# A squared-ReLU MLP in eight steps, with its two projections interleaved on TensorE

## The chip, the cores and the metric

The kernel runs on one core of one Trainium2 chip. The metric is the device time of one execution in microseconds (us); less is better. Engines are named as in the profile: PE (TensorE, matrix products), PEld (its weight loads), DVE (VectorE), ACT (ScalarE), POOL (GpSimd) and SP (SyncE, which issues the weight loads from memory).

## What is computed

A decoder trunk of two layers on 256 rows of 2,048 values, in float32. The change concerns the MLP, which each layer has once:

```python
D_MODEL = 2048; SEQ = 256; D_FF = 4 * D_MODEL          # 8,192 hidden values

def sq_relu_mlp(u, w_up, w_down):
    return jnp.square(jax.nn.relu(u @ w_up)) @ w_down

# in each layer, after the convolution or attention sub-layer:
u = rmsnorm(h, mlp_pre_g[i])
h = h + rmsnorm(sq_relu_mlp(u, mlp_w_up[i], mlp_w_down[i]), mlp_post_g[i])
```

Layer 0 has a gated short convolution ahead of its MLP, layer 1 a stick-breaking attention. These parts are the same in both kernels.

## The kernel before

**Float32 by parts.** Each operand is split into a rounded high part and the rest, its low part. A product of two operands takes three TensorE products: high x high, high x low and low x high. Weights come from memory in chunks of 128 x 1,024 (`raw`, four buffers, loads issued by SP). ACT rounds a chunk to `whi` (L144) and DVE subtracts to get `wlo` (L155). High and low parts go round in a ring of seven buffers each (`RING`), so a chunk's parts can be made ahead of PE by as much as the ring holds: a new part waits until PE has done with the one seven places before.

**Who sets the order.** PE executes the products in the order in which the program writes them. For DVE and ACT a scheduler decides the order when the kernel is built, except around the norms between sub-layers, where it is written out. An engine executes its instructions strictly in that order. On-chip result memory has eight banks of 128 x 512 values, and the building layer keeps two engines from touching one bank at the same time by adding waits.

**Up projection, by tiles.** `up` makes hidden tiles of 128 hidden values x 256 rows. For each of 16 blocks of the inner dimension there is one high product (L927: weights' high part, against the high and low parts of the input side by side, 512 columns) and one low product (L940: weights' low part against the input's high part, 256 columns, added to the first half of the bank). When a tile's 32 products are done, `hidden` copies the second half of the bank with ACT (`half`, L873), adds it to the first half with DVE (`s`, L875), and applies ReLU and square on ACT (L876, L877). The result is split into `hid` parts (L228, L229). Even tiles run all high products and then all low ones, odd tiles the other way round; the banks rotate over all eight. The first six tiles of an MLP (`LEAD_UP`) advance together, block by block.

**Down projection, by units.** For each 128 hidden values, and each half of the output columns, there are two row blocks x two column blocks of 512, three TensorE products each (`Group.half`, L281 to L283). `Mixed` replaces some pairs of neighbouring blocks of hidden values by a scheme with seven instead of eight products of sub-blocks (each three TensorE products; L348 to L350). It needs differences of the weights (`split_seven`, four DVE subtractions, L181), so that three and a half chunks are split for such a pair in place of two, and sums of the hidden tiles (`sums_of`). Four extra banks (`more`) collect products that belong to several outputs. When a group ends, ACT copies them out (L997) and nine accumulating DMAs issued by GpSimd (L989) add them to the output sums `mg`; in the last quarter DVE adds them (`combined`).

**The staging.** An MLP goes in four quarters of 2,048 hidden values. A quarter first makes all its 16 hidden tiles, then runs the down projection for both column halves. `PAIRS` names the pairs that take seven products: four for each column half in three quarters, two in the last. At the end of each quarter the sums are added to `mg` in memory on chip (L982, L984).

Of the kernel before, what the change touches and what calls it, by code (L numbers as in the profile page):

```python
# [14 lines left out]
P = 128  # L15
D = 2048
T = 256
# [29 lines left out]
QUARTERS = FF // D  # L47
PAIRS = ([(2, 5, 8, 11)] * 2, [(2, 5, 8, 11)] * 2, [(2, 5, 8, 11)] * 2, [(2, 6)] * 2)
APART = 11
# [10 lines left out]
UP_FIRST = lead_then_rows(list(range(KD)), LEAD_UP)  # L60
UP_ORDER = lead_then_rows(list(range(KD)), 0)
# [6 lines left out]
def trunk(ctx, tc, x, xT, vecs, rows, ws, out):  # L68
# [237 lines left out]

    class Mixed(Group):

        def __init__(self, first, xs, banks, evict, sums, extra, combine, pool, pairs):
            super().__init__(first, KD, xs, banks, evict)
            self.sums, self.extra, self.combine, self.pairs = sums, extra, combine, pairs
            self.more = None  # L320
            for i in pairs:
                sevens[first + i] = pool

        def both(self, i):
            if i in self.pairs:
                self.seven(i)
            elif i - 1 not in self.pairs:
                super().both(i)

        def seven(self, i):  # L330
            b11, b21, b22, t1, t2, t3, t4 = chunk(self.first + i)
            if self.more is None:
                self.more = [bank(n, "more") for n in self.extra]
            s1, more = self.sums[i]

            def x(k, b):
                return [part_of(self.xs, i + k, b, j) for j in range(2)]

            def sums(j):
                return [t[:, (j - 1) * P : j * P] for t in more] if j else s1  # L340

            p1, p5, p6, p7 = self.more
            for ps, (xh, xl), (hi, lo), own in (
                (p1, x(0, 0), b11, True), (self.ps[0, 0], x(1, 0), b21, False), (self.ps[0, 1], sums(3), b22, False),
                (p5, sums(0), t1, True), (p6, sums(1), t2, True), (p7, sums(2), t3, True),
                (self.ps[1, 0], x(1, 1), t4, False),
            ):
                nc.tensor.matmul(ps[:], xh, hi, start=own and i == self.pairs[0], stop=False)  # L348
                nc.tensor.matmul(ps[:], xh, lo, start=False, stop=False)  # L349
                nc.tensor.matmul(ps[:], xl, hi, start=False, stop=own and i == self.pairs[-1])  # L350
            if i == self.pairs[-1]:
                self.combine(*self.more)
            spent(UNIT * 7 / 4)
            spent(UNIT * 7 / 4)
# [338 lines left out]
    def mlp_weights(i):  # L693
        for q in range(QUARTERS):
            W["up", i, q] = Weights(ws[f"up{i}{q}"])
            W["dn", i, q] = Weights(ws[f"dn{i}{q}"])
# [168 lines left out]
    def mlp(pool, i, before, after):  # L865
# [5 lines left out]
        def hidden(xs, n, ps, sums, pairs):  # L871
            half = pool.tile([P, T], F32, tag="half", name="half", bufs=2)
            nc.scalar.activation(half[:], ps[:, T:], AF.Copy)  # L873
            s = pool.tile([P, T], F32, tag="s", name="s", bufs=3)
            nc.vector.tensor_tensor(s[:], ps[:, :T], half[:], op=ALU.add)  # L875
            nc.scalar.activation(s[:], s[:], AF.Relu)  # L876
            nc.scalar.activation(s[:], s[:], AF.Square)  # L877
            if xs[n // 4] is None:
                xs[n // 4] = operand("hid4")
            if n in pairs and n != APART:  # L880
                two_parts([part_of(xs, n, 0, j) for j in range(2)], s[:, :P])
            else:
                split_tile(xs, n, s[:])
            if n in pairs:
                held[n] = s
            elif n - 1 in pairs:
                sums[n - 1] = sums_of(xs, n - 1, held.pop(n - 1), s)

# [5 lines left out]
        def sums_of(xs, n, x, y):  # L894

            t = after.dump()
            s1, s2, s3, s4 = (t[:, j * P : (j + 1) * P] for j in range(4))
            a11, a21, a12, a22 = x[:, :P], x[:, P:], y[:, :P], y[:, P:]
            for to, u, v, op in (
                (s1, a21, a22, ALU.add), (s2, s1, a11, ALU.subtract),  # L900
                (s3, a11, a21, ALU.subtract), (s4, a12, s2, ALU.subtract),
            ):
                nc.vector.tensor_tensor(to, u, v, op=op)
            if n == APART:
                one = pool.tile([P, 2 * P], F32R, tag="s1", name="sums", bufs=1)
                one = [one[:, j * P : (j + 1) * P] for j in range(2)]
            else:
                one = [part_of(xs, n, 1, j) for j in range(2)]
            more = pool.tile([P, 6 * P], F32R, tag="hg", name="sums", bufs=4)
            more = [more[:, j * 3 * P : (j + 1) * 3 * P] for j in range(2)]  # L910
            two_parts(one, s1)
            two_parts(more, t[:, P:])
            return one, more

        def up(q, xs, sums, pairs):
            w = W["up", i, q]
            order = UP_FIRST if q == 0 else UP_ORDER
            place = {kn: m for m, kn in enumerate(order)}
            pss = {}

            def high(k, n, b=None, begin=True, end=False):

                if n not in pss:
                    pss[n] = bank((n + 2) % 8, "up")
                ps, x = pss[n][:].rearrange("p (a b t) -> p a b t", a=2, b=NB), u[k // 4][:, k % 4]
                if b is None:
                    nc.tensor.matmul(  # L927
                        ps, weight(0, k, n), x, start=begin and k == 0, stop=end and k == KD - 1, skip_group_check=end
                    )
                else:  # L930
                    nc.tensor.matmul(ps[:, :, b, :], weight(0, k, n), x[:, :, b, :], start=k == 0 and b == 0, stop=False)  # L931
                if end and k == KD - 1:
                    hidden(xs, n, pss.pop(n), sums, pairs)
                spent(TILE_HIGH if b is None else TILE_LOW)

            def low(k, n, begin=False, end=True):
                if n not in pss:
                    pss[n] = bank((n + 2) % 8, "up")
                x = u[k // 4][:, k % 4, 0].rearrange("p b t -> p (b t)")
                nc.tensor.matmul(  # L940
                    pss[n][:, :T], weight(1, k, n), x, start=begin and k == 0, stop=end and k == KD - 1,
                    skip_group_check=begin,
                )
                if end and k == KD - 1:
                    hidden(xs, n, pss.pop(n), sums, pairs)
                spent(TILE_LOW)

            def weight(part, k, n):
                m = place[k, n]
                return chunk(w.base + m // CH, part == 1)[part][:, m % CH * P : (m % CH + 1) * P]  # L950

            def tiles_of(kns):
                for k, n in kns:
                    high(k, n)
                for k, n in kns:
                    low(k, n)

            lead = list(range(LEAD_UP if q == 0 else 0))
            if lead:
                first = [(k, n) for k in range(ALONE) for n in lead]  # L960
                for b in range(NB):
                    for k, n in sorted(first, key=lambda kn: (kn[0] // 4, kn[1] // 3 if kn[0] < 4 else 0)):
                        high(k, n, b)
                for k, n in first:
                    low(k, n)
                for k in range(ALONE, KD):
                    tiles_of([(k, n) for n in lead])
            for n in range(len(lead), KD):
                if n % 2 == 0:
                    tiles_of([(k, n) for k in range(KD)])  # L970
                else:
                    for k in range(KD):
                        low(k, n, True, False)
                    for k in range(KD):
                        high(k, n, None, False, True)

        def add(q, j, c, b, ps, adds):
            r = part[b][2 * j + c]
            with tc.high_priority():
                if r is None:  # L980
                    r = part[b][2 * j + c] = result()
                    nc.scalar.activation(r, ps[:], AF.Copy)  # L982
# [4 lines left out]
            elif b and c:  # L987
                for first, second in adds:
                    nc.gpsimd.dma_start(first(), second, accum_op=ALU.add)  # L989
# [323 lines left out]
```

## Time and profile before

| | |
|---|---|
| Time, median of three runs | 2140.67 us (2140.43 to 2142.43) |
| Profiled execution | 2141.22 us, span of its trace 2139.5 us |
| Granted TensorE clock | 0.999 |
| Busy: PE, DVE, ACT, POOL | 99%, 73%, 63%, 5% of the span |
| Memory traffic | 194 GB/s read over the span |

The profile is one execution taken by the hardware profiler. Its groups give a line of the kernel, an engine, an operation, its output and inputs, a count, then busy time and the mean duration in ns, then the idle time before it and what ended that. Products on PE overlap: a product of 512 columns is listed with some 390 ns although the next may start earlier, so slots are read from the distance of starts. A list of waits gives total time, times and longest.

### The profile page before, as it was taken

How to read it: one execution, taken by the hardware profiler on the slowest of the kernel's cores; microseconds unless marked ns; L12 is line 12 of the kernel's file. 1: busy time of each engine (PE TensorE's matmuls, PEld its weight loads, DVE VectorE, ACT ScalarE, POOL GpSimd, SP SyncE). 2: the span in 40 equal slices, each digit the busy share in tenths (PEclk: the TensorE clock that was granted, in tenths of full speed). 3: DMA queues.
4: the chain of work that ended last, by engine and by line, in shares of the span. 5: the costliest groups of instructions: out<-in, count | busy, mean ns of one | idle time of the engine just before them, and what ended most of it. 6: DMA issues, size and time to landing. Idle time of an engine off the chain costs nothing.

```text
span 2139.5 us, 29677 instructions
## 1 busy us (share of the span) xinstructions
PE 2128.4 (99%) x10906; PEld 1822.7 (85%) x10906; DVE 1572.3 (73%) x2243; ACT 1340.6 (63%) x2010; POOL 100.1 (5%) x121
## 2 busy tenths in 40 slices
PE   9999999999999999999999999999999999999998
PEld 8888888888888888888888888889888888888886
DVE  8766655888679679768866777558886797687677
ACT  7545444766666666665567888547666666666654
POOL 0000000001101101100000000000011011011000
PEclk9999999999999999999999999999999999999999
DMA  8655664659858858965575445655588589569663
GB/s 306 216 187 187 189 234 145 218 178 257 247 175 248 263 171 243 268 207 171 176 231 168 158 158 171 214 166 188 183 250 261 172 236 276 186 205 287 213 198 121
DMA packets 130321, 445.54 MB, mean 208 GB/s; under 512 B 14592, under 2 KB 14848, under 8 KB 129152
## 3 DMA queue, kind: packets, MB, share of 16 engines
q1 hardware_dynamic: 113472, 408.65, 58.7%
q0 software_dynamic: 16416, 34.61, 8.3%
q8 instruction: 85, 1.39, 0.3%
q14 instruction: 60, 0.49, 0.1%
q10 hardware_dynamic: 288, 0.39, 0.1%
HBM read 413.19 MB, written 2.10 MB: 194 GB/s over the span
## 4 chain that ended last, share of the span: by engine, by line
PE 97%; ACT 1%; DVE 1%; DMA 1%; issue 0%; SPq 0%; DVEq 0%; ACTq 0%
PE up L927 21%; PE acc L281 12%; PE acc L283 12%; PE acc L282 12%; PE up L940 11%; PE acc L750 11%; PE more L348 2%; PE more L349 2%; PE more L350 2%; PE acc L348 2%; PE acc L349 2%; PE acc L350 2%; PE lead L750 2%; PE up L931 1%; PE tr L234 1%
## 5 line engine op out<-in xcount | busy, mean ns | idle before, releaser
L155 DVE TENSOR_TENSOR wlo<-raw,whi 128x1024 fp32r<-128x1024 f32 (+1 forms) x566 | 676.5, 1210 | 294.1 <-ACT whi L144 248.1
L144 ACT ACTIVATE whi<-raw 128x1024 fp32r<-128x1024 f32 (+1 forms) x566 | 590.6, 1048 | 296.8 <-PE acc L283 123.6
L927 PE MATMUL up<-u,whi 128*128 128x512 f32 x1952 | 458.3, 390 | 0.0
L927 PEld LDWEIGHTS up<-u,whi 128*128 128x128 f32 x1952 | 361.6, 188 | 71.7
L940 PEld LDWEIGHTS up<-u,wlo 128*128 128x128 f32 x2048 | 255.9, 191 | 5.8
L940 PE MATMUL up<-u,wlo 128*128 128x256 f32 x2048 | 259.0, 283 | 0.0
L281 PE MATMUL acc<-whi,hid 128*128 128x512 f32 x576 | 224.2, 389 | 0.0
L283 PE MATMUL acc<-whi,hid 128*128 128x512 f32 x576 | 224.1, 389 | 0.0
L282 PE MATMUL acc<-wlo,hid 128*128 128x512 f32 x576 | 224.1, 389 | 0.0
L157 DVE SCALAR_TENSOR_TENSOR wlo<-raw,gv,whi 128x512 fp32r<-128x512 f32 (+1 forms) x160 | 132.0, 853 | 41.6 <-ACT whi L144 41.0
L750 PE MATMUL acc<-u,whi 128*128 128x512 f32 x672 | 156.5, 390 | 0.0
L144 ACT ACTIVATE whi<-raw,gv 128x512 fp32r<-128x512 f32 (+1 forms) x160 | 121.7, 800 | 51.3 <-PE acc L283 35.2
L281 PE MATMUL acc<-whi,u 128*128 128x512 f32 x384 | 153.1, 399 | 0.1
L283 PE MATMUL acc<-whi,u 128*128 128x512 f32 x384 | 149.9, 390 | 0.0
L282 PE MATMUL acc<-wlo,u 128*128 128x512 f32 x384 | 149.7, 390 | 0.0
L750 PEld LDWEIGHTS acc<-u,whi 128*128 128x128 f32 x672 | 124.8, 188 | 25.0
L281 PEld LDWEIGHTS acc<-whi,hid 128*128 128x128 f32 x576 | 108.1, 188 | 22.5
L283 PEld LDWEIGHTS acc<-whi,hid 128*128 128x128 f32 x576 | 108.1, 188 | 22.5
L282 PEld LDWEIGHTS acc<-wlo,hid 128*128 128x128 f32 x576 | 108.1, 188 | 22.3
L876 ACT ACTIVATE s<-s 128x256 f32<-128x256 f32 x128 | 52.0, 412 | 84.9 <-DVE s L875 84.5
L229 DVE TENSOR_TENSOR hid<-s,hid 128x256 fp32r<-128x256 f32 x106 | 44.7, 424 | 75.4 <-ACT hid L228 75.3
L989 POOL DMA_DIRECT2D mg<-more x96 | 84.2, 984 | 256.5 <-DMA mg<-more 169.1
(2893 smaller groups left out, 3229.3 us busy)
## 6 DMA issues: line engine op xcount, KB each, us to landing
raw<-w_up SPq DMA_DIRECT2D x256, 512.0 KB, 4.5
raw<-w_dn SPq DMA_DIRECT2D x256, 512.0 KB, 4.2
raw<-w_in SPq DMA_DIRECT2D x94, 512.0 KB, 4.1
mg<-more POOLq DMA_DIRECT2D x96, 256.0 KB, 7.5
raw<-w_out SPq DMA_DIRECT2D x32, 512.0 KB, 3.7
raw<-w_v SPq DMA_DIRECT2D x32, 512.0 KB, 4.4
raw<-w_k SPq DMA_DIRECT2D x32, 512.0 KB, 4.0
raw<-w_q SPq DMA_DIRECT2D x32, 512.0 KB, 3.9
```

Of the source, the lines that this page charges most:

```text
L144: rounded = nc.scalar.activation(hi[:, at], raw[i][:, at], AF.Copy, scale=1.0 if gain is None else gain)
L155: nc.vector.tensor_tensor(lo[:, at], t[:, at], hi[:, at].bitcast(F32), op=ALU.subtract)
L157: nc.vector.scalar_tensor_tensor(lo[:, at], t[:, at], gain, hi[:, at].bitcast(F32), op0=ALU.mult, op1=ALU.subtract)
L281: nc.tensor.matmul(ps[:], xh, hi[:, a], start=i == 0 and k == 0, stop=False)
L282: nc.tensor.matmul(ps[:], xh, lo[:, a], start=False, stop=False)
L283: nc.tensor.matmul(ps[:], xl, hi[:, a], start=False, stop=i == self.n - 1 and k == self.ks - 1)
L348: nc.tensor.matmul(ps[:], xh, hi, start=own and i == self.pairs[0], stop=False)
L349: nc.tensor.matmul(ps[:], xh, lo, start=False, stop=False)
L350: nc.tensor.matmul(ps[:], xl, hi, start=False, stop=own and i == self.pairs[-1])
L750: nc.tensor.matmul(ps[:, :cols], w, xs[:, :cols], start=k == 0 and part == parts[0], stop=k == KD - 1 and part == parts[1], skip_group_che ...
L927: nc.tensor.matmul(ps, weight(0, k, n), x, start=begin and k == 0, stop=end and k == KD - 1, skip_group_check=end)
L940: nc.tensor.matmul(pss[n][:, :T], weight(1, k, n), x, start=begin and k == 0, stop=end and k == KD - 1, skip_group_check=begin,)
```

## The change

The MLP goes in eight steps of 1,024 hidden values. After the eight hidden tiles of the first step, every hidden tile of the next step (32 products) is followed by one pair of the down projection of the present step, so the two projections alternate on PE. Weights come in the order in which they are then used (`step_chunks`), as one array per step.

- Three of four pairs in both column halves take seven products in steps 0 to 6; in the last step one pair does (`SEVEN`): 43 of 64 pairs in each MLP, 28 before.
- All up tiles after the first eight use one bank (`UP_BANK`, 2). All tiles run high products first. The ACT copy of the bank's second half (`half_of`) now stands between a tile's high and low products.
- The output sums have fixed banks (`DOWN_BANKS`). In an eight-product pair the sum (1, 1) uses the up tiles' bank and is added to `mg` at once. The other sums collect over eight pairs, one column half over the end of a step and the start of the next.
- The extra products are added by the same accumulating DMAs (`add_later`), at the end of the MLP by DVE (`add_now`).
- The last step's second half is a plain `Group` of eight units, followed by the same end as before.

```diff
-QUARTERS = FF // D
-PAIRS = ([(2, 5, 8, 11)] * 2, [(2, 5, 8, 11)] * 2, [(2, 5, 8, 11)] * 2, [(2, 6)] * 2)
+STEPS = 8
+UP_BANK = 2
+DOWN_BANKS = {(0, 0): 3, (0, 1): 4, (1, 0): 5, (1, 1): UP_BANK, 1: 6, 5: 7, 6: 0, 7: 1}
+SEVEN = [((1, 2, 3), (1, 2, 3))] * 7 + [((0,), ())]
...
-            for n in range(len(lead), KD):
-                if n % 2 == 0:
-                    tiles_of([(k, n) for k in range(KD)])
-                else:
-                    for k in range(KD):
-                        low(k, n, True, False)
-                    for k in range(KD):
-                        high(k, n, None, False, True)
+        def half_of(n):
+            halves[n] = pool.tile([P, T], F32, tag="half", name="half", bufs=2)
+            nc.scalar.activation(halves[n][:], pss[n][:, T:], AF.Copy)
+
+        def whole_up(to, n, first, number):
+            for k in range(KD):
+                high(first, k, k, n, number)
+            half_of(n)
+            for k in range(KD):
+                low(first, k, k, n)
+            finish(to, n)
...
+            for k in range(ALONE, KD):
+                for n in lead:
+                    high(first, place[k, n], k, n, n + 2)
+                for n in lead:
+                    if k == KD - 1:
+                        half_of(n)
+                    low(first, place[k, n], k, n)
+                    if k == KD - 1:
+                        finish(to, n)
...
+                for c in range(2):
+                    self.products((0, c), "sum", at, [factors(0, c, t) for t in range(2)])
+                self.products((1, 1), own, at, [factors(1, 1, t) for t in range(2)])
+                if own == at:
+                    add(self.j, 1, 1, self.ps.pop((1, 1)))
+                self.products((1, 0), "sum", at, [factors(1, 0, t) for t in range(2)])
...
+        for e in range(STEPS):
...
+            new = Hidden(e + 1)
+            for h in range(2):
+                if e == 0 or h == 1:
+                    plan = [(e, m, h) for m in range(4)]
+                    if h == 1:
+                        plan += [(e + 1, m, 0) for m in range(4)]
+                    down = Down(band_of(e, h), plan)
+                for m in range(4):
+                    at_chunk = first + 16 * h + 4 * m
+                    whole_up(new, 4 * h + m, at_chunk, UP_BANK)
+                    down.pair((e, m, h), at_chunk + 2, now)
+            now = new
```

More of the change, by code (lines that the diff above doesn't have):

```diff
@@ L305, in last_units @@
                     spent(UNIT / 2)
[L307 to L354, printed above, removed]
     def run(groups, enter=False, leave=None):
@@ new lines, in mlp, with weight, high @@
+        pss, halves = {}, {}
+        def weight(part, first, m):
+            return chunk(first + m // CH, part == 1)[part][:, m % CH * P : (m % CH + 1) * P]
+        def high(first, m, k, n, number, b=None):
+            if n not in pss:
+                pss[n] = bank(number, "up")
+            ps, x = pss[n][:].rearrange("p (a b t) -> p a b t", a=2, b=NB), u[k // 4][:, k % 4]
+            if b is None:
+                nc.tensor.matmul(ps, weight(0, first, m), x, start=k == 0, stop=k == KD - 1)
+            else:
+                nc.tensor.matmul(ps[:, :, b, :], weight(0, first, m), x[:, :, b, :], start=k == 0 and b == 0, stop=False)
+            spent(TILE_HIGH if b is None else TILE_LOW)
@@ L1044, in mlp @@
                 turned["banks"] = [2, 3]
-            up(q, xs, sums, pairs[0])
-            run(groups, leave=after if last else None)
+                for m in range(4):
+                    down.pair((e, m, 0), first + 2 * m, now)
+                run(
+                    [Group(first + 8, 8, now.xs, LAST_BANKS, lambda b, c, ps: add(band_of(e, 1), b, c, ps, True))],
+                    leave=after,
+                )
+                break
+            new = Hidden(e + 1)
+            for h in range(2):
+                if e == 0 or h == 1:
[3 more added lines that the diff above has]
+                    down = Down(band_of(e, h), plan)
+                for m in range(4):
+                    at_chunk = first + 16 * h + 4 * m
+                    whole_up(new, 4 * h + m, at_chunk, UP_BANK)
+                    down.pair((e, m, h), at_chunk + 2, now)
+            now = new
     def sublayer_pool(name, post, pre):
```

307 lines of the change are left out of this document (168 added, 139 removed).

## The prediction

> **What bounds the kernel now.** I read the page's head first, then the list of who waited for whom on TensorE (PE), then the chain that ended last.
>
> ```profile
> span 2139.5 us, 29677 instructions
> PE 2128.4 (99%) x10906; PEld 1822.7 (85%) x10906; DVE 1572.3 (73%) x2243; ACT 1340.6 (63%) x2010; POOL 100.1 (5%) x121
> PE 97%; ACT 1%; DVE 1%; DMA 1%; issue 0%; SPq 0%; DVEq 0%; ACTq 0%
> ...
> PE warm L740 <- DVE ones L85: 1.1, 1, 1.1
> PE tr L234 <- DVE h L510: 0.7, 2, 0.4
> PE lead L750 <- ACT whi L144: 0.3, 1, 0.3
> ```
>
> PE is busy for 99% of the span and waits three times, none of them in an MLP. So the time is PE's list of products laid end to end. A product taken out of an MLP is worth its whole slot, and a wait put in front of one costs its whole length, because PE has no spare time in which to absorb it.
>
> ```profile
> 600.00:690.00 90.00, 90.00 (x429) 75.82 (x428) 77.16 (x100) 56.79 (x76) 7.88 (x9) 1.00 0.74 214
> 690.00:780.00 90.00, 90.00 (x500) 78.88 (x499) 60.45 (x85) 58.78 (x95) 7.88 (x9) 1.00 0.78 234
> ```
>
> These are two stretches of an MLP (after the stretch: PE, weight loads, VectorE, ScalarE, GpSimd, then clock and DMA share). PE is full in both and its clock is 1.00; VectorE (DVE) has 77 of 90 us in the first, so it is next in line.
>
> **What a product costs.** The first rows below are from the timeline of the down projection, the last two from the chain in order of time, where a row is a run of products.
>
> ```profile
> 638.08 0.39 PE L348 MATMUL more<-whi229a,hid 128*128 128x512 f32 x1
> ...
> 642.84 0.39 PE L281 MATMUL acc<-whi,hid 128*128 128x512 f32 x1
> ...
> 599.45 7.28 PE up L927 x32
> 610.56 7.28 PE up L927 x32
> ```
>
> From 638.08 to 642.84 PE issued the 21 products of one seven-product pair: 4.76 us, 0.2267 each (their 0.39 overlap, so a product still runs 0.16 after its slot). A pair with eight products has 24, 5.44 us. In the up projection 32 high products take 7.28 us (0.2275 each), and the 32 high and 32 low products of two tiles take 610.56 - 599.45 = 11.11, so a tile takes 5.56 (high 3.64, low 1.92).
>
> **Part 1: fewer products.** Each MLP has 64 pairs. Before, 28 take seven products (3 x 2 x 4 + 2 x 2); after, 43 (7 x 6 + 1). 15 more in each of two MLPs, three TensorE products fewer each: 90 x 0.2267 = **-20.4 us**. The built order agrees: 90 fewer products, nothing else of PE's changed in number.
>
> **Part 2: a wait in every up tile.** Before, a tile's high and low products ran in one go and only then ScalarE (ACT) copied the upper half of its bank (`half`, L873). After, `whole_up` issues 16 high products, then the copy `half_of`, then 16 low products into the lower half of the *same* bank. In the built order of the changed kernel the first low product of each of the 128 up tiles waits for ACT's count, and that count is reached by exactly this tile's copy:
>
> ```
> PE L916 Matmult up_8630<-u4_3406,wlo320_8525
>      waits Activation => ACT L912 Activation half_8665<-up_8630
> ```
>
> Columns don't overlap, but the order is kept for the bank. [...]
>
> What a wait costs is in these rows, the last up tile of a quarter and then the only kind of place where PE waits in mid-kernel:
>
> ```profile
> 624.71 0.62 PE L927 MATMUL up<-u,whi 128*128 128x512 f32 x2
> 625.16 0.39 PE L281 MATMUL acc<-whi,hid 128*128 128x512 f32 x1
> 625.36 0.38 ACT L873 ACTIVATE half<-up 128x256 f32<-128x256 f32 x1 [0.75 <-PE up L927]
> 625.79 0.42 DVE L875 TENSOR_TENSOR s<-up,half 128x256 f32<-128x256 f32 x1
> ...
> 1048.22 0.75 DVE L510 SCALAR_TENSOR_TENSOR h<-mg,rstd,h 128x512 f32<-128x512 f32 x1
> 1049.03 0.66 PE L234 MATMUL tr<-ident,h 128*128 128x128 f32 x4 [0.41 <-DVE h L510]
> ```
>
> The last high products end at 624.71 + 0.62 = 625.33; ACT, idle and waiting, starts the copy at 625.36 and ends it at 625.74; PE meanwhile issued its next product at 625.16. With the wait, PE could go on no sooner than 625.74. Its own wake is in the last rows: DVE ended at 48.97 and PE began at 49.03, 0.06 later; I add as much again for a weight load that can't run ahead (an estimate from the same 0.06). So a tile loses 625.74 - 625.16 + 0.12 = 0.70, taken as 0.69 with rounding; from below it is 0.58 (nothing but the copy), from above 0.58 + 0.42 = 1.0, where PE's wake is as long as the whole 0.41 for which it stood idle there. I take 0.69, since each piece has a row. 64 - 6 = 58 tiles per MLP go through `whole_up`: 116 x 0.69 = **+80.0 us** (+67 to +116).
>
> Is the copy ever late? In ACT's order the piece before it is mostly the next tile's second weight piece (`whi`, L144), whose ring slot comes free after eight high products: 1.82 us, plus 0.19 for tail and start, plus 1.06 for the piece = 3.07 into the tile. The copy can't start before 3.64 + 0.19 = 3.83. So ACT is there 0.76 early, and I add nothing.
>
> ```profile
> L144 ACT ACTIVATE whi<-raw 128x1024 fp32r<-128x1024 f32 x558 | 587.9, 1057 | 295.4 <-PE acc L283 123.6 <-DMA raw<-w_up 48.3 <-PE acc L750 37.8
> L877 ACT ACTIVATE s<-s 128x256 f32<-128x256 f32 x128 | 52.4, 416 | 3.4
> L876 ACT ACTIVATE s<-s 128x256 f32<-128x256 f32 x128 | 52.0, 412 | 84.9 <-DVE s L875 84.5
> L873 ACT ACTIVATE half<-up 128x256 f32<-128x256 f32 x128 | 47.8, 380 | 67.6 <-PE up L927 34.8 <-PE up L940 32.6
> L891 ACT ACTIVATE sums<-sq 128x384 fp32r<-128x384 f32 x28 | 14.4, 513 | 0.0
> ```
>
> **Part 3: the six leading tiles.** They finish together: six last high products, then per tile a copy and one low product. ACT's order has copies 0 and 1, a weight piece, then ReLU, square and rounding of tiles 0 and 1, and only then copies 2 and 3; copy 4 comes after one more ReLU, copy 5 behind ten more short pieces. PE's six low products (0.72 us in all) stand in that order too, so the chain is ACT's: from the last high product 0.2 + 1.0 (weight piece) + 6 x 0.35 + 2 x 0.33 (copies 2, 3), 0.4 for DVE's sum of tile 2, 0.7 (ReLU, copy 4), 3.2 (ten pieces), 0.33 (copy 5) = 8.6, and about 0.2 for the last product. I count a 0.41 piece as 0.35 because pieces without a dependence start before the one ahead has ended. 8.8 - 0.72 = 8.1 us per MLP, twice: **+16.2 us** (+4 if only the copies count, +20 at full durations).
>
> **Part 4: what lies beside PE.** DVE gets 282 more instructions (2,245 to 2,527 in the built order), most of them in splitting weight sums. Take half a step: four up tiles, one eight-product pair, three seven-product pairs; PE needs 22.2 + 5.4 + 14.3 = 42.0 us, and with part 2 44.7. DVE by the rows below and full durations: 19 x 1.222 + 15 x 0.683 + 2.5 evictions x 0.681 = 35.2; hidden tiles 4 x 0.417 for the sums, about 1.5 for the low parts and 3.0 for the tile sums: 41.3. So it fits, with 3.4 us over; the DVE work is costed at nothing as long as PE's waits cover it.
>
> ```profile
> L155 DVE TENSOR_TENSOR wlo<-raw,whi 128x1024 fp32r<-128x1024 f32 x558 | 673.6, 1222 | 292.9 <-ACT whi L144 246.9 <-PE up L940 18.8 <-issue 13.2
> L181 DVE TENSOR_TENSOR sums<-raw,sums 128x512 f32<-128x512 f32 x112 | 76.5, 683 | 0.1
> L984 DVE TENSOR_TENSOR mg<-mg,acc 128x512 f32<-128x512 f32 x48 | 31.2, 681 | 8.0 <-PE acc L283 7.8
> L875 DVE TENSOR_TENSOR s<-up,half 128x256 f32<-128x256 f32 x128 | 52.9, 417 | 0.0
> DVE hid L229 <- ACT hid L228: 75.3, 67, 2.4
> raw<-w_up SPq DMA_DIRECT2D x256, 512.0 KB, 4.5
> L989 POOL DMA_DIRECT2D mg<-more x96 | 84.2, 984 | 256.5 <-DMA mg<-more 169.1 <-DVE mg L984 58.9 <-ACT mg L982 20.2
> ```
>
> ACT needs about 31 of these 44.7 us. SP issues the same number of loads, one per 2.8 us against 2.55 in the down projection before (16 in 8 x 2.72 + 4 x 4.76 = 40.8), so the loads' 4.5 us stay hidden with four buffers. GpSimd's accumulating DMAs rise from 108 to 126, still nine per group; nobody on PE's path waits for them. Up tiles and the (1, 1) sum of an eight-product pair now share bank 2: PE returns to it 6 x 0.2267 = 1.36 us after that sum's last slot, and its eviction takes 0.16 + 0.68 + 0.1. In DVE's order 1.8 to 3.0 us of work stand between the up tile and this eviction (4.4 twice), while the sum is complete 18 x 0.2267 + 0.16 = 4.2 us after the tile, so I count 0; with one long DVE piece ahead each time it would be up to 0.7 late, 28 x 0.7 = +20.
>
> **Sum.** -20.4 + 80.0 + 16.2 = +75.8 us on the profiled execution of 2141.22 (span 2139.5 and 1.7 around it): 2217.0. The median before is 2140.67, 0.55 less, so I forecast **2216.5 us**. What a measurement here can tell from no change is about 0.2%, 4.3 us.
>
> **The rivals.**
> *The copies come late* (0.12). If ACT falls 0.76 us behind, each copy stands behind a weight piece. A third of a piece, 0.35, at 116 tiles adds 41 us: 2257. For it: more ACT work around group ends (four copies of 0.59). Against it: 14 us free per half-step.
> *DVE becomes the bound* (0.06). Before, DVE stood 75.3 / 67 = 1.1 us at a time for a hidden tile's rounding. With 1.1 at all four tiles a half-step takes 41.3 + 4.5 = 45.8, 1.1 over PE's 44.7; 28 half-steps: +31, 2247. Against it: in the new order other pieces stand between sum and rounding.
> *The waits are free* (0.04). If weights' low parts reached PE later than the copy anyway, or ACT's copy were done when PE arrives, only part 1 would be left: 2120, faster. It decides below 20.4 / 116 = 0.18 us a tile. Against it: the copy needs the last high product, which ends after PE's next slot.
> *The clock drops* (0.05). A gap of 0.7 us every 5 us is new here. PE's slowest product, at the start, took 796 ns against a median of 395:
>
> ```profile
> L750 PE MATMUL lead<-u,whi x96: 387/395/796, 5.0 to 39.3; 128*128 128x512 f32 x96
> ```
>
> If a tenth of the two MLPs' PE time (2 x 675 us) ran at half speed, +135 us: 2352. [...]
>
> **Chances.** Forecast 0.73, rivals as given. Range: 2141 - 20 + 67 + 4 = 2192 below, taken as 2190; above, late copies and some of the bank-2 waits, 2265. The free waits and the clock lie outside, and so may a tenth of the rest. Faster 0.03, same 0.01 (waits nearly free), slower 0.96.
>
> **What would show it.** PE idle near 96 us, nearly all at the low products' line and released by `half`; about 0.69 us per tile; two stretches of some 8 us at the end of the leading tiles; 90 products fewer; clock 1.00. Wrong if PE shows no waits for `half`, if they are over 1 us each, or if DVE or a DMA ends most of PE's idle time.

## The result and the profile after

| | before | after |
|---|---|---|
| Time, median | 2140.95 us (2140.43 to 2142.43, 4 runs) | 2324.16 us (2318.87 to 2328.08, 4 runs) |
| Profiled execution, its span | 2141.22 us, 2139.5 us | 2328.08 us, 2326.4 us |
| Granted TensorE clock | 0.999 | 0.977 |

The change makes the kernel slower: 1.0853 times the time before, 95% interval 1.0829 to 1.0877. That is +183 us where +75.8 was forecast, and the time lies above the forecast range of 2190 to 2265 us.

The head of the page, its chain that ended last, and the list of PE's waits, of the changed kernel:

```profile
span 2326.4 us, 29793 instructions
PE 2177.3 (94%) x10816; PEld 1824.8 (78%) x10816; DVE 1723.4 (74%) x2525; ACT 1381.2 (59%) x2108; POOL 116.4 (5%) x139
...
PE 79%; DMA 8%; ACT 6%; DVE 4%; issue 2%; SPq 0%; DVEq 0%; ACTq 0%
```

```profile
PE up L916 <- ACT half L912: 120.8, 124, 5.2
PE up L905 <- DVE mg L961: 9.2, 2, 4.7
PE up L905 <- ACT mg L959: 8.8, 2, 4.8
```

PE has 90 products fewer, 10816, as counted. Its share of the span falls from 99% to 94%, and DMA, ACT and DVE, with about 1% each of the chain before, now hold 18%. The waits are where they were expected, at the low products' line L916 for the copy `half`. But the longest is 5.2 us, not 0.7, and there are four waits of up to 4.8 us that the forecast counted as nothing, for the eviction of the (1, 1) sum in the shared bank. The two stretches of the MLP shown for before now read:

```profile
600.00:690.00 90.00, 80.88 (x400) 67.29 (x400) 69.79 (x99) 50.38 (x78) 7.93 (x9) 0.96 0.65 196
690.00:780.00 90.00, 81.48 (x393) 67.68 (x392) 69.37 (x99) 52.87 (x81) 7.90 (x9) 0.96 0.66 203
```

PE was busy for 90 of 90 us and is now for 81. No other engine is full (DVE 70, ACT 50), so this is not an engine that became the bound but PE waiting in between; and the clock, 1.00 before, is 0.96.

**A normal tile and a late one.** In PE's timeline of the changed kernel the first two rows are a tile's high and low products in the common case. The next two are the first tile after the end of a group of output sums, which stands ahead of the eight-product pair that opens the next group:

```profile
704.93 3.79 PE L905 MATMUL up<-u,whi 128*128 128x512 f32 x16
709.19 2.17 PE L916 MATMUL up<-u,wlo 128*128 128x256 f32 x16 [0.47 <-ACT half L912]
...
664.73 3.79 PE L905 MATMUL up<-u,whi 128*128 128x512 f32 x16
673.50 3.78 PE L916 MATMUL up<-u,wlo 128*128 128x256 f32 x16 [4.99 <-ACT half L912]
```

From the first high to the first low product it is 4.26 us where 3.64 is the products' own time: 0.62 for the wait. The low products then take 2.01 to the next pair instead of 1.92. So a normal tile loses 0.71 us; 0.69 was forecast. The late tile's low products begin 8.77 us after its first high one, 4.5 us later than normal. Its low products are listed with 3.78 us instead of 2.17, in a stretch (670.76 to 677.59) in which the granted clock was 0.50.

**Why the copy is late there.** The chain in order of time, then ACT's order, both at that tile (start, duration, what):

```profile
661.85 1.27 DVE mg L961 x2
...
663.97 1.15 DVE wlo L174
...
665.17 6.87 DMA raw<-w_mlp
...
672.12 1.06 ACT whi230b L208
673.18 0.28 ACT half L912
673.46 0.04 issue
673.50 3.78 PE up L916 x16
```

```profile
667.15 0.64 ACT L208 ACTIVATE whi230a<-raw 128x512 fp32r<-128x512 f32 x1
672.12 1.06 ACT L208 ACTIVATE whi230b<-raw 128x1024 fp32r<-128x1024 f32 x1 [4.33 <-DMA raw<-w_mlp]
673.08 0.37 ACT L912 ACTIVATE half<-up 128x256 f32<-128x256 f32 x1
```

The copy's input is complete at about 668.5 (664.73 + 3.79), but in ACT's order it stands behind `whi230b`, the rounding of weights for the *next* seven-product pair, which PE uses only from 689.8 on, by that piece's rows in the trace. That piece waits for a load. The load could not start before a `raw` buffer was free; the buffer was freed by DVE's `wlo` at 665.1, itself behind the evictions at the end of the group (`mg`). The load then took 6.87 us, not 4.5; the 16 DMA engines were busy all that time (a share of 1.08 from 665.1 to 672.0, against 0.65 over the stretch shown above). In ACT's rows the copy begins only behind that piece: ACT stood idle until 672.12, for the last 3.6 us of it with the copy's input ready behind.

### The profile page after: what moved, and what is told of

It reads as the page before. It is cut to its first block, busy times and chain, and to the rows that moved or that the text cites. A ratio compares the mean times of both kernels' runs of the same rounds, so it can differ in the third digit from the quotient of the medians.

```text
span 2326.4 us, 29793 instructions
## 1 busy us (share of the span) xinstructions
PE 2177.3 (94%) x10816; PEld 1824.8 (78%) x10816; DVE 1723.4 (74%) x2525; ACT 1381.2 (59%) x2108; POOL 116.4 (5%) x139
## 4 chain that ended last, share of the span: by engine, by line
PE 79%; DMA 8%; ACT 6%; DVE 4%; issue 2%; SPq 0%; DVEq 0%; ACTq 0%
PE up L905 15%; PE up L916 10%; PE acc L719 10%; DMA raw<-w_mlp 8%; PE acc L300 7%; PE acc L302 7%; PE acc L301 7%; PE acc L1008 4%; PE acc L1009 4%; PE acc L1010 4%; PE more L1008 3%; PE more L1009 3%; PE more L1010 3%; DVE wlo L174 2%; ACT half L912 2%
## 5 line engine op out<-in xcount | busy, mean ns | idle before, releaser
L174 DVE TENSOR_TENSOR wlo<-raw,whi 128x1024 fp32r<-128x1024 f32 (+1 forms) x506 | 606.7, 1208 | 246.7 <-ACT whi L163 171.4
L163 ACT ACTIVATE whi<-raw 128x1024 fp32r<-128x1024 f32 (+1 forms) x506 | 526.4, 1047 | 232.6 <-PE acc L302 84.0
L916 PE MATMUL up<-u,wlo 128*128 128x256 f32 x2048 | 297.8, 299 | 120.8 <-ACT half L912 120.8
L916 PEld LDWEIGHTS up<-u,wlo 128*128 128x128 f32 x2048 | 269.0, 200 | 173.4 <-ACT half L912 172.2
L200 DVE TENSOR_TENSOR sums<-raw,sums 128x512 f32<-128x512 f32 x172 | 117.9, 685 | 1.6
L200 DVE TENSOR_TENSOR sums<-raw,raw 128x512 f32<-128x512 f32 x86 | 58.9, 685 | 49.3 <-DMA raw<-w_mlp 49.3
L719 PEld LDWEIGHTS acc<-u,wlo 128*128 128x128 f32 x672 | 83.5, 192 | 1.7
L912 ACT ACTIVATE half<-up 128x256 f32<-128x256 f32 x128 | 48.2, 380 | 61.6 <-PE up L905 61.5
L302 PEld LDWEIGHTS acc<-whi,u 128*128 128x128 f32 x384 | 72.1, 188 | 15.6
L719 PE MATMUL acc<-u,wlo 128*128 128x256 f32 x672 | 84.2, 283 | 0.0
L1008 PE MATMUL acc<-whi,hid 128*128 128x512 f32 x204 | 83.4, 409 | 0.0
```

The source lines that it names most:

```text
L163: rounded = nc.scalar.activation(hi[:, at], raw[i][:, at], AF.Copy, scale=1.0 if gain is None else gain)
L174: nc.vector.tensor_tensor(lo[:, at], t[:, at], hi[:, at].bitcast(F32), op=ALU.subtract)
L200: nc.vector.tensor_tensor(t, x, y, op=ALU.subtract)
L302: nc.tensor.matmul(ps[:], xl, hi[:, a], start=False, stop=i == self.n - 1 and k == self.ks - 1)
L719: nc.tensor.matmul(ps[:, :cols], w, xs[:, :cols], start=k == 0 and part == parts[0], stop=k == KD - 1 and part == parts[1], skip_group_che ...
L916: nc.tensor.matmul(pss[n][:, :T], weight(1, first, m), x, start=False, stop=k == KD - 1, skip_group_check=True)
```

## The experiments

The theory at this point (A in most expectations): a normal tile costs the forecast 0.71 us; the excess over the forecast comes from short pieces on PE's path (copy, sum, eviction) that stand in ACT's and DVE's order behind weight pieces of seven-product pairs, which wait for loads. The rival (B): the interleaving itself, the gaps, the clock or the loads cost the time, whatever that order is.

### Where the copy stands

**Both kinds of tile with the copy behind the low products.**

```diff
             for k in range(KD):
                 high(first, k, k, n, number)
-            half_of(n)
             for k in range(KD):
                 low(first, k, k, n)
+            half_of(n)
             finish(to, n)
```

(and the same in the leading tiles)

> Edit: in every up tile the copy of the bank's upper half stands behind the low products again (in the leading six tiles too); all else as changed. Theory A (the loss is the wait for this copy, in three prices: 0.71 us at each of 116 tiles, 8 to 9 us at each lead, and longer ones where the copy itself is late, with the half-clock spells that follow): all of it goes and the 90 products fewer remain, 2120 us (2118 to 2132), PE waiting less than 15 us in all and the clock back at 1.00. Theory B (DVE's and the loads' chain is the bound of the interleaved stage, and the copy is only where it shows): the wait moves to the weight parts in the down pairs, 2180 us or more.

Measured: 2160.84 us (2154.34 to 2161.93), 1.0088 of before [1.0075, 1.0102], 163 us less than the changed kernel. Neither number was met. All waits for the copy are gone. What is left over 2120 is for the most part these waits of 22 us, besides four stretches, the first from 462.9 to 465.7, in which products of 512 columns start 0.43 us apart instead of 0.23:

```profile
PE more L1007 <- DVE s L859: 16.7, 15, 2.7
PE up L905 <- DVE mg L960: 5.2, 8, 0.7
```

The first is the (1, 1) product of an eight-product pair, which needs the up tiles' bank and so the up tile's sum `s`. So nearly everything hangs on the copy's place. The rest shows at the bank that the two projections share; why, the last group of runs tells.

**The leading tiles alone, and the others alone.** The same edit only in the leading tiles, and only in the 116 whole tiles.

> Edit: only in the six leading tiles of each MLP does the copy stand behind the low products. Theory A: two waits of 8.4 us and some 10 us at half clock behind each go: 2324 - 17 - 6 = 2301 us (2294 to 2310). Theory B: the lead lies ahead of the interleaved stage, whose DVE chain then starts no earlier: 2316 to 2326.

Measured: 2320.41 us (2315.78 to 2322.92), about 4 less than the changed kernel, whose runs overlap with these. Theory A missed, and the number is theory B's.

> The changed kernel with the copy behind the low products in the 116 whole tiles, but between them in the twelve leading tiles, as the change has it. Theory A (the leading tiles' stall is a term of its own): 2160.8 + 2 x 8.4 = 2178 (2172 to 2188, with halved clock after each stall at the upper end). Theory B (the stall only moves time that would be lost right after, as the run with the leading tiles alone changed seemed to say): 2161 to 2168.

Measured: 2179.63 us (2178.54 to 2181.23), 18.8 more than with all copies behind: theory A, so the leading tiles do have a price of their own. The two results fit together by these rows of PE's timeline, the leading tiles' end with the copies between there (the last run), and the first whole tile when only the leading tiles were changed:

```profile
396.23 1.55 PE L905 MATMUL up<-u,whi 128*128 128x512 f32 x6
399.00 0.66 PE L916 MATMUL up<-u,wlo 128*128 128x256 f32 x2 [1.22 <-ACT half L912]
402.59 0.85 PE L916 MATMUL up<-u,wlo 128*128 128x256 f32 x2 [2.93 <-ACT half L912]
404.41 0.58 PE L916 MATMUL up<-u,wlo 128*128 128x256 f32 x1 [0.97 <-ACT half L912]
407.79 0.58 PE L916 MATMUL up<-u,wlo 128*128 128x256 f32 x1 [2.80 <-ACT half L912]
```

```profile
399.81 3.82 PE L905 MATMUL up<-u,whi 128*128 128x512 f32 x16
411.95 0.58 PE L916 MATMUL up<-u,wlo 128*128 128x256 f32 x1 [8.32 <-ACT half L912]
```

The leading tiles' chain on ACT holds PE up for about as long either way: 7.92 us in the four waits of the first rows, 8.32 in the one of the second. When the leading tiles did not wait for it, the next tile's copy stood behind it. The stall went only where neither waited.

### The wait without the interleaving

**The kernel before, with the copy between high and low products in its 116 whole tiles.**

```diff
             def tiles_of(kns):
                 for k, n in kns:
                     high(k, n)
+                if len(kns) == KD:
+                    half_of(kns[0][1], pss[kns[0][1]])
                 for k, n in kns:
                     low(k, n)
...
-                if n % 2 == 0:
+                if True:
                     tiles_of([(k, n) for k in range(KD)])
```

> The kernel before, with one thing of the change alone: all hidden tiles after the leading six run high products first and the ACT copy stands between high and low products, in 116 tiles over both MLPs (58 in each); the two projections are not interleaved and the banks still rotate over eight. Theory A (the wait itself costs 0.6 to 0.7 us a tile wherever it stands; what is late in the changed kernel comes from seven-product pairs standing right behind the tiles): 2140.7 + 116 x 0.71 = 2223 (2205 to 2240), nearly all of PE's idle time released by the copy, few copies later than 1 us, clock above 0.99. Theory B (any such gap brings spells of halved clock and late loads, the order of the projections does not matter): over 2270, clock below 0.985.

Measured: 2248.33 us (2248.1 to 2250.47), 1.0503 [1.0488, 1.0519], clock 0.995. Two tiles of PE's timeline, and the first whole tile of the first MLP:

```profile
565.39 3.82 PE L934 MATMUL up<-u,whi 128*128 128x512 f32 x16
569.68 2.17 PE L947 MATMUL up<-u,wlo 128*128 128x256 f32 x16 [0.47 <-ACT half L875]
571.70 3.82 PE L934 MATMUL up<-u,whi 128*128 128x512 f32 x16
...
398.63 3.82 PE L934 MATMUL up<-u,whi 128*128 128x512 f32 x16
409.81 3.79 PE L947 MATMUL up<-u,wlo 128*128 128x256 f32 x16 [7.36 <-ACT half L875]
```

A tile takes 6.31 us instead of 5.56: 0.75, and 114 x 0.75 = 86. The rest of the 107 us are two waits of 7.4 behind the leading tiles' pieces, which A's number did not have and therefore missed by 8 at its upper end, and slower products after each (above, 3.79 us for the 16 low ones instead of 2.17). B's number is farther off, and outside these two no copy is late. So the wait has its price without interleaving too, but the late copies belong to the interleaved order.

### The order repaired, the waits kept

**Weight roundings of seven-product pairs behind the copy.** In ACT's order only; `issue_after` puts a rounding behind the last copy written ahead of it:

```diff
-            nc.scalar.activation(hi[:, at], src, AF.Copy)
...
+                with tc.issue_after(last_copy[0].ins):
+                    nc.scalar.activation(hi[:, at], src, AF.Copy)
```

> Edit: the rounding of a seven-product pair's weights on ACT is ordered behind the last copy, so that no copy stands behind a weight piece that waits for its load; the copy itself stays between high and low products. Theory A: the 28 copies ahead of eight-product pairs fall from 2.3 us on average to 0.62, 28 x 1.7 = 47 us, and most half-clock spells with them, some 15 us: 2262 us (2250 to 2285). Theory B: the load is as late as before and the wait goes to the pair's weight parts: 2310 to 2330.

Measured: 2267.44 us (2263.2 to 2272.22): theory A. By PE's starts, the 28 tiles ahead of an eight-product pair now pay 1 us in all beyond the normal wait, where they paid 50. With 57 us gone, the list of PE's waits is:

```profile
PE up L921 <- ACT half L917: 71.9, 124, 3.4
PE up L910 <- DVE mg L966: 13.6, 7, 5.4
PE up L910 <- ACT mg L964: 7.4, 2, 3.8
```

**On ACT behind the copy and on DVE behind the tile's sum.** `behind("half")` and `behind("s")` put an instruction behind the last copy or the last sum written ahead of it.

```diff
+            with behind("s"):
                 nc.vector.tensor_tensor(t, x, y, op=ALU.subtract)
...
+            with behind("half"):
                 nc.scalar.activation(hi[:, at], src, AF.Copy)
+            with behind("s"):
                 low_part(hi, lo, src, at, None)
```

> The changed kernel with its copies where it has them, between high and low products, and one edit: ACT's rounding and DVE's subtractions for a seven-product pair's weights are put behind the copy and the sum of the hidden tile written before them. Theory A (what the prediction lacked is only that copy and sum stand behind these pieces, which stand behind loads): the prediction's own terms are left, 2120 + 116 x 0.71 + 2 x 8.4 = 2219, with some halved clock after the two long waits 2216 to 2240; no wait for the copy over 1 us outside the leading tiles, PE's waits for the (1, 1) eviction below 8 us. Theory B (the gaps themselves lower the clock or delay loads): 2250 to 2268, with several spells of halved clock in mid-MLP.

Measured: 2265.68 us (2262.92 to 2267.55). Theory A missed by 26 at its upper end, and the number lies in theory B's range. But outside the leading tiles slower products come only behind the four long waits for the eviction (3.62 to 4.48 us), where the next high products are listed with 5.36 to 6.52 us instead of 3.79. The copies are in time; these waits have stayed, and ACT's order shows why (the same place of the first group):

```profile
472.00 0.65 ACT L216 ACTIVATE whi166a<-raw 128x512 fp32r<-128x512 f32 x1
480.66 1.06 ACT L216 ACTIVATE whi166b<-raw 128x1024 fp32r<-128x1024 f32 x1 [8.01 <-DMA raw<-w_mlp]
...
483.67 0.58 ACT L968 ACTIVATE mg<-more 128x512 f32<-128x512 f32 x1
```

The piece that waits for its load now stands behind the copy, and the eviction of the (1, 1) sum stands behind the piece. At the next change of groups the eviction is DVE's, and there it stands behind DVE's pieces for the same weights, which waited for their load up to 576.08.

**And that sum in another bank.** In the pair that opens a group:

```diff
-                    self.ps[key] = bank(DOWN_BANKS[key], "acc" if own == "sum" else "more")
+                    number = DOWN_BANKS[1 if own == self.plan[0] else key]
+                    self.ps[key] = bank(number, "acc" if own == "sum" else "more")
```

> The kernel of 2265.68 (the change with its copies in their place; weight pieces of seven-product pairs behind copy and sum) and one more edit: the eight-product pair that opens a group of output sums puts its sum (1, 1) in a bank of the extra sums. Theory A (what is over the prediction's terms is that sum's eviction, which stands behind a weight piece that waits for its load, and the halved clock after it): the four waits of 3.8 to 4.7 us and the halved products behind them go, 26 + 9 us: 2231 (2224 to 2240), with halved clock only after the two stalls of the leading tiles. Theory B (the piece that waits for its load delays something else then): the wait turns up at the next tile's copy or sum, 2248 or more.

Measured: 2245.62 us (2244.45 to 2246.89), between the two theories' numbers, and 29 above the forecast of 2216.5. The waits for the eviction shrink from 22.0 us in total to 2.3:

```profile
PE up L925 <- ACT half L921: 78.3, 124, 3.4
PE up L914 <- DVE mg L970: 2.3, 12, 0.2
```

but the wait for the copy rises by 7.4, most of it at the four next tiles (2.0 and 2.6 us in the first MLP). In the first of them ACT works off without a pause, from 479.5 to 485.8, what the piece that waited for its load had held up, and the copy is at the end of that. So the piece that waited for its load delayed the copy here, as it had delayed the eviction there.

### A pair between high and low products

**The seven-product pair moved between the tile's high and low products**, so that PE has work while ACT copies.

```diff
-                    whole_up(new, 4 * h + m, at_chunk, UP_BANK)
-                    down.pair((e, m, h), at_chunk + 2, now)
...
+                    if m in SEVEN[e][h]:
+                        for k in range(KD):
+                            high(at_chunk, k, k, n, UP_BANK)
+                        half_of(n)
+                        down.pair((e, m, h), at_chunk + 2, now)
+                        for k in range(KD):
+                            low(at_chunk, k, k, n)
+                        finish(new, n)
...
```

> Edit: where a seven-product pair follows an up tile, the pair stands between the tile's high and low products, so the copy lies beside the pair's products; tiles ahead of an eight-product pair stay as changed. Theory A: 84 of the 116 waits of 0.71 us go, 60 us; the late copies ahead of eight-product pairs stay: 2264 us (2250 to 2285). Theory B: 2310 to 2330, since PE would only wait elsewhere for DVE.

Measured: 2321.52 us (2318.22 to 2324.94), no gain: theory B. The copy's wait is hidden in these tiles, and a new one takes its place, since the next tile's high products need the same bank right after the low ones, before DVE has made the sum:

```profile
PE up L905 <- DVE s L859: 75.9, 82, 1.7
PE up L916 <- ACT half L912: 68.4, 40, 4.9
```

### What was left with the copies behind

These start from the kernel of 2160.84 us.

**The (1, 1) sum last in an eight-product pair** (its two lines moved behind those of (1, 0)).

> The changed kernel with the copies behind the low products (2160.84 measured) and one more edit: in an eight-product pair the sum (1, 1), which shares the up tiles' bank, comes last instead of third. Theory A (what is left over 2120 is the bank that up tiles and the sum (1, 1) share): the wait of the (1, 1) products for the up tile's sum (16.7 us) goes nearly away, since 1.36 us more of products lie ahead, but the next up tile now waits for the eviction, 0.16 + 0.68 + 0.1 = 0.94 us in each of 28 pairs, 26 us: 2150 to 2175, no better. Theory B (what is left are late weights, whatever the bank): 2158 to 2163 with the waits at the same lines as before.

Measured: 2172.69 us (2167.98 to 2175.29): theory A. The wait moves to the next up tile, which now stands right behind the eviction in the shared bank: `mg` on DVE releases 24 waits of PE, 23.2 us, close to the estimated 0.94 each.

**The (1, 1) sum in another bank where the pair opens a group** (the edit shown above).

> The changed kernel with the copies behind the low products (2160.84 measured) and one more edit: the eight-product pair that opens a group of output sums (16 of 28 over both MLPs) puts its sum (1, 1) in a bank of the extra sums, which is free then, instead of the up tiles' bank. Theory A (the shared bank makes the rest): the four longest waits (3.9 to 4.4 us each, all in such pairs) go, about 17 us, and about half of the rest: 2130 to 2146. Theory B (late weights): over 2155.

Measured: 2155.55 us (2153.2 to 2158.4): a gain of 5 only, which is within the spread of the runs: B's number. PE's waits say which reading is right:

```profile
PE up L905 <- DVE s L859: 15.4, 7, 3.9
PE more L1008 <- DVE s L859: 5.7, 7, 1.0
```

The sum `s` is as late as before, and now the next up tile waits for it. So the bank only tells who waits; that the sum is late has another cause. DVE's order in the kernel of 2160.84 shows it:

```profile
457.79 0.69 DVE L200 TENSOR_TENSOR sums<-raw,raw 128x512 f32<-128x512 f32 x1 [3.22 <-DMA raw<-w_mlp]
...
461.88 0.68 DVE L174 TENSOR_TENSOR wlo166a<-raw,whi166a 128x512 fp32r<-128x512 f32 x1
462.48 0.41 DVE L859 TENSOR_TENSOR s<-up,half 128x256 f32<-128x256 f32 x1
```

**Weight pieces of seven-product pairs behind copy and sum** (the edit shown above).

> The changed kernel with the copies behind the low products (2160.84 measured) and one more edit: ACT's rounding and DVE's subtractions for a seven-product pair's weights are put behind the copy and the sum of the hidden tile written before them, so that these no longer stand behind the pair's loads. Theory A (the rest is the shared bank, late because the tile's sum stands behind weight pieces in DVE's order): the 16.7 us of waits of the (1, 1) products go to under 5, 2122 to 2145. Theory B (the weights then come too late themselves): PE waits for weight pieces instead, 2155 or more.

Measured: 2129.68 us (2128.48 to 2130.03), 0.9946 of before [0.993, 0.9963]: theory A. No wait for `s` is left, and ten of up to 0.9 us for the eviction.

**Both.**

> The kernel of 2129.68 (copies behind the low products; weight pieces of seven-product pairs behind copy and sum) and one more edit: the eight-product pair that opens a group of output sums puts its sum (1, 1) in a bank of the extra sums. Theory A (the rest over 2120 is the shared bank, 0.6 us in each of ten pairs, and half or more of these pairs open a group): 2121 to 2128. Theory B (those waits are in the pairs in the middle of a group): 2128.5 to 2132, the ten waits of up to 0.9 us for the (1, 1) eviction as before.

Measured: 2121.15 us (2120.61 to 2121.78), 0.9907 of before [0.9893, 0.9922]. This is the fastest version: 0.9% below the kernel before, clear of its interval, and theory A. Its span, its engines and the second stretch of its MLP:

```profile
span 2119.4 us, 29769 instructions
690.00:780.00 90.00, 90.00 (x458) 76.98 (x458) 80.88 (x116) 62.41 (x95) 7.90 (x9) 1.00 0.79 228
```

PE is full again, at a clock of 1.00; 20.1 us under before's span is the whole of part 1. DVE, with 81 of 90 us, would be next.

## Why the prediction was right or wrong

**Part 1 was right.** -20.4 us was forecast; the version without waits is 20.1 us below before.

**Part 2 was right in its price.** 0.71 us per tile against 0.69, so 82 us against 80.0. The kernel before with this wait alone paid 0.75.

**Part 3 was nearly right.** PE's timeline of the changed kernel, the last six high products of the leading tiles and the first whole tile behind them:

```profile
396.52 1.55 PE L905 MATMUL up<-u,whi 128*128 128x512 f32 x6
...
408.61 5.09 PE L905 MATMUL up<-u,whi 128*128 128x512 f32 x16
```

After 6 x 0.2275 for the high products, 408.61 - 396.52 - 1.36 = 10.7 us go by, in which there are 0.7 us of low products: 10.0 are lost, 9.3 in the second MLP. That is 19.3, of which 15.5 are PE's waits and the rest restarts behind them and halved clock (a granted clock of 0.50 from 401.1 to 411.4), against 16.2, within the bound of 20. Like the copy's price it comes from ACT's order, with the leading tiles' pieces in it.

**The step that failed is "Is the copy ever late? ... I add nothing".** It looked at a copy behind the next tile's ordinary weight piece (L144 before), and there its 0.76 us of slack held: the 88 whole tiles that are not ahead of an eight-product pair pay 0.62 or a little more, apart from halved clock in six. At 22 of the 28 ahead of one, ACT has pieces of a seven-product pair in front of the copy that still wait for loads. The 28 pay 50 us above their 28 x 0.62 (worked out from PE's starts, as for the late tile above). The rival "the copies come late" named the right engine and place, but with a third of a piece, 0.35 us, at all tiles; it was up to 4.7 us at a quarter of them. With the roundings behind the copy alone these 50 us go but for 1, and the time falls by 57, so this cause is shown.

**Two zeros of part 4 failed with it.** "The loads' 4.5 us stay hidden with four buffers": at a change of groups they don't, since a load starts only when DVE has freed a buffer, behind the evictions, and took 6.87 us there. And the (1, 1) evictions were counted 0, up to 20 at 0.7 each; they cost 18.8, in four places. The price was not an evictor's own time, but the pieces ahead of it for the same weights that waited for a load: on ACT in two of the places and on DVE in the other two.

**The clock rival held in part.** The forecast was a clock of 1.00, with 0.05 for a drop. In the trace after there are 17 stretches at a granted clock of 0.50 in the kernel's middle, of 3.4, 6.8 or 10.2 us. The rows are intervals of 3.41 us (PE's busy time comes first, the clock third from the end), an interval with a wait and the one behind it, twice; then the sum of all 17 stretches:

```profile
817.54:820.95 3.41, 1.63 (x14) 1.56 (x14) 3.27 (x7) 2.39 (x3) 0.00 (x0) 1.00 0.52 208
820.95:824.36 3.41, 3.41 (x13) 2.82 (x12) 2.98 (x4) 1.25 (x3) 0.00 (x0) 0.50 0.69 217
...
964.31:967.72 3.41, 1.64 (x13) 1.64 (x14) 2.50 (x4) 2.33 (x3) 0.87 (x1) 1.00 1.07 247
967.72:971.13 3.41, 3.41 (x19) 2.88 (x18) 2.77 (x4) 1.15 (x3) 0.87 (x1) 1.00 1.07 338
...
sum 102.00, PE 78.92 PEld 68.83 DVE 67.27 ACT 46.59 POOL 17.50; mean PE 4.64 PEld 4.05 DVE 3.96 ACT 2.74 POOL 1.03
```

PE was busy in 78.9 of them, so about half of that, 39 us, is lost; 26 of these are seen directly in high and low products that took longer than normal, and 8 more in eight-product pairs behind a late tile.

But the cause is not the one that the rival named. Short gaps at every tile did not lower the clock by themselves: before with the copy between has 114 of them, of 0.65 us (569.68 - 565.39 - 3.64, by its rows above), and its only such stretches in the middle are the two that follow its two waits of 7.4 us. Its mean clock is 0.995, where the changed kernel has 0.977. Nor did the length of one wait tell: a wait of 1.78 us was followed by such a stretch (the first two rows), and one of 3.43 was not (the last two).

The clock records of the changed kernel show more. All 17 stretches begin and end on one grid of 3.413 us, to within 0.01 us, wherever the waits begin. In the interval of that grid ahead of each of the 17, PE stood idle for 1.78 us or more; in every other interval at full clock in the middle it was 1.78 or less. The wait of 3.43 lay across two intervals, with 1.66 and 1.77 us of it. This is what one trace shows; that idle time in such an interval is what lowers the clock was not tried by a run of its own.

**The account.** Against the 2119.4 us span of the version without waits, the changed kernel's 2326.4 are 207.0 more: 82 for normal waits, 19 for the leading tiles, 50 for late copies, 19 for the (1, 1) evictions, 34 for products at half clock (26 in up tiles, 8 in eight-product pairs), 2 in seven-product pairs. That is 206. The first two are the prediction's terms, 101 against 96.2; the other 105 are what it missed, nearly all of the 107.7 between forecast and result. These terms are read from the trace; the runs that keep the waits and repair the order took 78.5 us of it away, down to 2245.62.

**What stays open.** Why the loads at the change of groups took 6.87 us and, at the first one, 9.45 was not tried apart. The accumulating DMAs run there too, and the DMA engines were full at both (shares of 1.08 and 1.03), which fits; but no run takes those DMAs away or gives `raw` more buffers.

## What to carry to other kernels

A short piece of another engine that is put into PE's path can take over the waits that stand ahead of it in that engine's order, as the copies did here (50 us at 28 tiles): look in the built order at what precedes it at *every* kind of place (group ends, the first tile of a kind), not at the most frequent one. Where something ahead of it waited for a load, the load's lateness became PE's, up to 5.2 us at a tile; put pieces for work that is far off behind it, which took 57 us away here. Where an expected gain of fewer products doesn't show, take the wait out before giving up the products: here the same 90 products gave 20 us as soon as nothing waited.

## What the hardware showed that was not expected

- In the changed kernel the granted clock fell to 0.50 for whole intervals of a grid of 3.413 us, each time after an interval in which PE was idle for 1.78 us or more; of the 17 stretches, 6 were of one interval, 9 of two and 2 (after the leading tiles) of three. In the late tile above the low products so took 3.58 us to the next pair. The stretches keep to one grid while the waits begin anywhere in it, so the waits' lengths alone did not tell their effects: after one of 1.78 us the clock fell, after one of 3.43 it did not.
- The low products behind a normal wait cost a little beyond it: 2.01 us for 16 in the changed kernel and 2.02 in before with the copy between, in place of 1.92.
